# Split products of a tile pair: both wide products first, then both narrow ones

## Chip, cores and metric

One core of a Trainium2 chip runs the whole program. The metric is the device time of one execution in microseconds. Before the change the median of 3 runs is 2590.49 us (2587.98 to 2591.93).

## What is computed

A trunk of two layers over 256 positions of width 2048, in float32. Layer 0 mixes tokens with a causal Conformer convolution, layer 1 with a Mamba-2 mixer; each mixer is followed by a squared-ReLU MLP of width 8192. Cut to what matters:

```python
h = x
for i in range(2):
    sh1, sc1, g1, sh2, sc2, g2 = split(silu(c) @ w_mod[i] + b_mod[i])
    u = rmsnorm(h, norm_mix_g[i]) * (1 + sc1) + sh1
    h = h + g1 * (conformer_conv(u, ...) if i == 0 else mamba2(u, ...))
    u = rmsnorm(h, norm_mlp_g[i]) * (1 + sc2) + sh2
    r = relu(u @ mlp_w1[i])
    h = h + g2 * ((r * r) @ mlp_w2[i])
return rmsnorm(h, final_norm_g)
```

Nearly all of the work is in the large matrix products: `mlp_w1`, `mlp_w2`, the Mamba input and output projections, the Conformer's two pointwise products and `w_mod`.

## The kernel before

Activations stand transposed: channels on the 128 partitions, the T = 256 positions along the row. To keep float32 accuracy with single-pass products, a weight `w` and an activation `x` are each split into a high part (rounded to the format `F32R`) and a low part (the rest). A split activation tile holds high and low side by side, `x[:, t, :T]` and `x[:, t, T:]`, 512 columns in all. A product of a 128x128 weight tile then takes two matmuls: a wide one, high weights times both halves (512 columns), and a narrow one, low weights times the high half (256 columns), added into the right half of the same PSUM bank. The two halves of the bank are added when it is read out.

`block` computes 512 output channels from 2048 input channels. It opens 4 banks (one for each column group of 128 outputs, index `j`), and goes through 4 weight tiles of 1 MB (index `g`), each of 4 tiles of 128 input channels. `load_w` streams such a tile through SyncE's queue into one of 3 buffers `w32`. `split_w` splits it in two parts (index `i`), each of two input tiles (index `k`): ScalarE casts the high part to `wh` (line 361, 128x1024), VectorE subtracts to get `wl` (line 363). `wh` and `wl` have 3 buffers each, so ScalarE can only go on when TensorE has done with an older one. For each part and each column group TensorE then runs the products of the two input tiles, `products(...)` for `k = 0` and `k = 1`. After the second and the fourth column group `self.step()` lets waiting small jobs issue (in the Mamba layer those of the scan). After the last part `evac` reads the bank out.

With `single=True` a block writes into one half bank only: high weights times high, high weights times low, low weights times high, three matmuls of 256 columns. `block_t` (lines 430 to 432) is a third kind, with the activations as stationary operand and the weights streamed: three matmuls of 512 columns for each step. `outer` runs several blocks in step and uses `products` with `single`.

`block` without `single` runs for 13 blocks of `mlp_w1` and 3 of `mlp_w2` in layer 0, 20 blocks of the Mamba input projection (`win`), 7 of its output projection (`wout`) and 13 blocks of `mlp_w1` in layer 1: 56 blocks of 64 products.

The order on each engine is set by a scheduler of the framework: it goes by the program's order, by priorities (`high_priority`) and by when an operand should be ready, so where a weight half comes late it may run a later column group first. Only SyncE's weight stream is kept in the program's order.

Of the kernel before, what the change touches and what calls it, by code (L numbers as in the profile page):

```python
# [16 lines left out]
T = 256  # L17
# [162 lines left out]
class Trunk:  # L180
# [147 lines left out]
    def pump(self, n):  # L328
        for _ in range(n):
            if self.jobs:  # L330
                self.gemv(*self.jobs.pop(0))
        for v in self.rows_left:
            v[-1] += 1
        if self.rows_left and self.rows_left[0][-1] > WAIT:
            self.columns()
# [36 lines left out]
    def products(self, bank, w, x, k, t, cs, single, start, stop):  # L372


        def mm(out, lhsT, rhs, **kw):
            self.pe = self.nc.tensor.matmul(out, lhsT=lhsT, rhs=rhs, skip_group_check=True, **kw).ins  # L376
# [5 lines left out]
        else:  # L382
            mm(bank, wh[:, k, cs], x[:, t, :], start=start, stop=False)
            mm(bank[:, T:], wl[:, k, cs], x[:, t, :T], start=False, stop=stop)

    def block(self, src, rhs, evac, pump=None, single=False, ahead=None, after=(None, None)):


        banks = [self.bank(self.mm, "mm") for _ in range(4)]
        if single:  # L390
            banks = [v[:, :T] for v in banks]
        for g in range(4):
            w = self.load_w(src[g])
            if pump:
                with nullcontext() if g else self.tc.issue_after(self.evac):
                    self.pump(pump(g))
            with self.tc.high_priority(self.ahead if ahead is None else ahead):
                parts = self.split_w(w, (), after if g == 0 else (None, None), after[1] if g == 0 else None)
            for i, hl in enumerate(parts):
                for j in range(4):  # L400
                    cs = slice(j * P, (j + 1) * P)
                    for k in range(2):
                        t = 2 * i + k
                        self.products(banks[j], hl, rhs[g], k, t, cs, single, g == 0 and t == 0, g == 3 and t == 3)
                    if g == 3 and i == 1:
                        evac(j, [banks[j]] if single else [banks[j][:, T:], banks[j][:, :T]])
                    if j % 2:
                        self.step()
# [972 lines left out]
```

## Time and profile before

| | |
|---|---|
| runs | 2591.93, 2590.49, 2587.98 us |
| profiled execution, first to last instruction | 2591.2 us |
| TensorE matmul busy | 2540.7 us |
| TensorE weight loads busy | 2184.0 us |
| VectorE busy | 1910.9 us |
| ScalarE busy | 1311.4 us |
| GpSimd busy | 147.0 us |
| mean TensorE clock granted | 0.990 |
| moved by DMA | 664.85 MB |

The page gives no time of the profiled execution besides its span, which lies within the range of the runs. Matmuls overlap: a row of the timeline has the start and the length of a matmul, and the length reaches into the following one, so the rate of TensorE is read from the distance of starts. In the chain of work that ended last, neighbouring instructions of a line are drawn together ("x512"), and the length of such a piece is what the stretch cost. Rows called PEld are the loads of a stationary operand, which run beside the matmuls.

### The profile page before, as it was taken

How to read it: one execution, taken by the hardware profiler on the slowest of the kernel's cores; microseconds unless marked ns; L12 is line 12 of the kernel's file. 1: busy time of each engine (PE TensorE's matmuls, PEld its weight loads, DVE VectorE, ACT ScalarE, POOL GpSimd, SP SyncE). 2: the span in 40 equal slices, each digit the busy share in tenths (PEclk: the TensorE clock that was granted, in tenths of full speed). 3: DMA queues.
4: the chain of work that ended last, by engine and by line, in shares of the span. 5: the costliest groups of instructions: out<-in, count | busy, mean ns of one | idle time of the engine just before them, and what ended most of it. 6: DMA issues, size and time to landing. Idle time of an engine off the chain costs nothing.

```text
span 2591.2 us, 36890 instructions
## 1 busy us (share of the span) xinstructions
PE 2540.7 (98%) x14671; PEld 2184.0 (84%) x14671; DVE 1910.9 (74%) x2460; ACT 1311.4 (51%) x2011; POOL 147.0 (6%) x212
## 2 busy tenths in 40 slices
PE   7999999999999999999999999999999999999998
PEld 5887698988888888888888888888998888888886
DVE  6579577877878878888777777898885555565565
ACT  2067453544434434447777667744454444443443
POOL 0011000000000000000000000000001101101000
PEclk8999999999999999999999999999999999999999
DMA  9988797788888878856555455688765555555553
GB/s 404 381 322 305 266 344 300 284 326 311 313 329 316 324 287 346 320 216 221 172 194 175 167 189 194 233 310 326 294 245 192 195 181 193 194 182 194 193 184 141
DMA packets 94895, 664.85 MB, mean 257 GB/s; under 512 B 10977, under 2 KB 10977, under 8 KB 16769
## 3 DMA queue, kind: packets, MB, share of 16 engines
q1 hardware_dynamic: 89138, 643.87, 67.4%
q0 software_dynamic: 5152, 16.97, 2.4%
q8 instruction: 115, 1.88, 0.3%
q10 hardware_dynamic: 432, 1.66, 0.2%
q14 instruction: 58, 0.48, 0.0%
HBM read 657.02 MB, written 2.20 MB: 254 GB/s over the span
## 4 chain that ended last, share of the span: by engine, by line
PE 93%; DVE 3%; DMA 2%; ACT 1%; issue 1%; POOL 0%; ACTq 0%; SPq 0%; DVEq 0%
PE mm L376 58%; PE mm L430 8%; PE mm L431 8%; PE mm L432 8%; PE mm L712 7%; DMA hid<-wmT 1%; PE mm L658 1%; DVE wl L363 1%; PE ms L712 1%; DMA wm<-wmT 1%; PE ms L1293 0%; PE ms L283 0%; DMA t<-eac_d 0%; DVE hid L292 0%; ACT wh L361 0%
## 5 line engine op out<-in xcount | busy, mean ns | idle before, releaser
L376 PE MATMUL mm<-u,wh 128*128 128x512 f32 (+1 forms) x4544 | 1376.5, 365 | 4.4 <-ACT u L485 2.3
L363 DVE TENSOR_TENSOR wl<-w,wh 128x1024 fp32r<-128x1024 f32 x768 | 942.2, 1229 | 506.1 <-ACT wh L361 500.3
L361 ACT CAST wh<-w 128x1024 fp32r<-128x1024 f32 x768 | 806.1, 1050 | 975.2 <-PE mm L376 589.5
L376 PE MATMUL mm<-u,wl 128*128 128x256 f32 x3840 | 1081.0, 282 | 0.1
L376 PEld LDWEIGHTS mm<-u,wh 128*128 128x128 f32 x4544 | 812.6, 190 | 156.1 <-issue 6.6
L376 PEld LDWEIGHTS mm<-u,wl 128*128 128x128 f32 x3840 | 730.5, 190 | 5.8 <-issue 2.5
L430 PE MATMUL mm<-wh,hid 128*128 128x512 f32 x896 | 351.0, 392 | 0.0
L432 PE MATMUL mm<-wh,hid 128*128 128x512 f32 x896 | 348.9, 389 | 0.0
L431 PE MATMUL mm<-wl,hid 128*128 128x512 f32 x896 | 348.8, 389 | 0.0
L292 DVE SCALAR_TENSOR_TENSOR wm<-wm,scb 128x2048 f32<-128x2048 f32 x132 | 301.7, 2286 | 11.4 <-DMA wm<-wmT 11.2
L712 PE MATMUL mm<-u,w 128*128 128x256 f32 x864 | 191.8, 383 | 18.7 <-ACT u L586 18.7
L712 PEld LDWEIGHTS mm<-u,w 128*128 128x128 f32 x864 | 164.7, 192 | 45.1 <-ACT u L586 19.9
L430 PEld LDWEIGHTS mm<-wh,hid 128*128 128x128 f32 x896 | 168.3, 188 | 35.8 <-issue 1.0
L431 PEld LDWEIGHTS mm<-wl,hid 128*128 128x128 f32 x896 | 168.3, 188 | 35.3 <-issue 0.7
L432 PEld LDWEIGHTS mm<-wh,hid 128*128 128x128 f32 x896 | 168.3, 188 | 35.1
L376 PE MATMUL mm<-hid,wh 128*128 128x512 f32 (+1 forms) x576 | 182.3, 373 | 0.0
L376 PE MATMUL mm<-hid,wl 128*128 128x256 f32 x512 | 144.1, 281 | 0.0
L292 DVE SCALAR_TENSOR_TENSOR hid<-hid,scb 128x2048 f32<-128x2048 f32 x44 | 100.5, 2287 | 41.7 <-DMA hid<-wmT 41.5
L376 PEld LDWEIGHTS mm<-hid,wh 128*128 128x128 f32 x576 | 104.1, 189 | 20.3 <-ACT u L485 0.2
L320 POOL TENSOR_TENSOR mod<-mod,par 128x4 f32<-128x4 f32 x46 | 37.1, 806 | 1128.8 <-DVE wm L292 915.2
L605 ACT ACTIVATE taps<-u,par 128x256 f32<-128x256 f32 x224 | 93.1, 500 | 9.2 <-DVE taps L614 6.7
L376 PEld LDWEIGHTS mm<-hid,wl 128*128 128x128 f32 x512 | 97.0, 190 | 0.4 <-issue 0.2
(251 smaller groups left out, 1606.0 us busy)
## 6 DMA issues: line engine op xcount, KB each, us to landing
w<-w SPq DMA_DIRECT2D x256, 1024.0 KB, 4.9
wm<-wmT SPq DMA_DIRECT2D x139, 1024.0 KB, 7.3
w<-win SPq DMA_DIRECT2D x80, 1024.0 KB, 4.9
hid<-wmT SPq DMA_DIRECT2D x53, 1024.0 KB, 10.5
w<-pw SPq DMA_DIRECT2D x46, 1024.0 KB, 6.9
w<-wout SPq DMA_DIRECT2D x32, 1024.0 KB, 6.9
acc<-ac_d POOLq DMA_DIRECT2D x16, 512.0 KB, 8.0
xpad<-u POOLq DMA_DIRECT2D x24, 131.5 KB, 8.1
```

The source lines that it names most:

```text
L292: self.sum = nc.vector.scalar_tensor_tensor(out=w, in0=w, scalar=1.0, in1=self.scb, op0=ALU.mult, op1=ALU.mult, accum_out=m[:, i:i + 1]).ins
L320: nc.gpsimd.tensor_tensor(out=m, in0=m, in1=b, op=ALU.add)
L361: nc.scalar.copy(out=wh, in_=w[:, s, :])
L363: nc.vector.tensor_tensor(out=wl, in0=w[:, s, :], in1=wh.bitcast(F32), op=ALU.subtract)
L376: self.pe = self.nc.tensor.matmul(out, lhsT=lhsT, rhs=rhs, skip_group_check=True, **kw).ins
L430: mm(banks[q], lhsT=hi, rhs=wh[:, k, :], start=g == 0 and t == 0, stop=False)
L431: mm(banks[q], lhsT=hi, rhs=wl[:, k, :], start=False, stop=False)
L432: mm(banks[q], lhsT=lo, rhs=wh[:, k, :], start=False, stop=g == 3 and t == 3)
L605: st["tap"] = nc.scalar.activation(out=p4[:, q, :], in_=vp[:, k + q:k + q + T], func=AF.Identity, scale=self.col("w_dw", ct * TAPS + k + q ...
L658: self.pe = nc.tensor.matmul(o[32 * c:32 * c + 32, :], lhsT=w[:, k, 32 * c:32 * c + 32], rhs=r[:, c, k:k + T], start=k == 0, stop=k == 7, ...
L712: self.pe = nc.tensor.matmul(o, lhsT=w[:, t, j * P:(j + 1) * P], rhs=u[g][:, t, :], start=g == 0 and t == 0 and j < 2, stop=g == 3 and t == 3,
```

## The change

In `block`, for blocks without `single`, the four matmuls of a column group and part come in another order: the two wide ones (`k = 0` and `k = 1`), then the two narrow ones. The flags that open and close the accumulation are adapted: the first wide one of the block opens the bank, the last narrow one closes it. Blocks with `single`, `outer` and `block_t` keep their order.

```diff
+    def one_sort(self, bank, w, x, k, t, cs, lows, start, stop=False):
+
+        if lows:
+            out, lhsT, rhs = bank[:, T:], w[1][:, k, cs], x[:, t, :T]
+        else:
+            out, lhsT, rhs = bank, w[0][:, k, cs], x[:, t, :]
+        self.pe = self.nc.tensor.matmul(out, lhsT=lhsT, rhs=rhs, start=start and not lows, stop=stop and bool(lows),
+                                        skip_group_check=True).ins
+
...
-                    for k in range(2):
-                        t = 2 * i + k
-                        self.products(banks[j], hl, rhs[g], k, t, cs, single, g == 0 and t == 0, g == 3 and t == 3)
+                    if single:
+                        for k in range(2):
+                            t = 2 * i + k
+                            self.products(banks[j], hl, rhs[g], k, t, cs, single, g == 0 and t == 0, g == 3 and t == 3)
+                    else:
+                        for lows in range(2):
+                            for k in range(2):
+                                self.one_sort(banks[j], hl, rhs[g], k, 2 * i + k, cs, lows,
+                                              g == 0 and i == 0 and k == 0, g == 3 and i == 1 and k == 1)
```

On TensorE, in a `mlp_w1` block of the last MLP, before. Each row is a matmul: line, output bank, activation tile `u`, weight half `wh` or `wl`, and the shape of the output:

```order
L376 MATMUL mm_19358<-u_16268,wh_19366 128x512
L376 MATMUL mm_19358<-u_16268,wl_19367 128x256
L376 MATMUL mm_19359<-u_16268,wh_19366 128x512
L376 MATMUL mm_19359<-u_16268,wl_19367 128x256
L376 MATMUL mm_19359<-u_16268,wh_19366 128x512
L376 MATMUL mm_19359<-u_16268,wl_19367 128x256
L376 MATMUL mm_19356<-u_16466,wh_19404 128x512
L376 MATMUL mm_19356<-u_16466,wl_19405 128x256
```

The same place after the change ("x2" is two alike in a row):

```order
L392 MATMUL mm_19358<-u_16268,wh_19366 128x512 x2
L392 MATMUL mm_19358<-u_16268,wl_19367 128x256 x2
L392 MATMUL mm_19359<-u_16268,wh_19366 128x512 x2
L392 MATMUL mm_19359<-u_16268,wl_19367 128x256 x2
L392 MATMUL mm_19356<-u_16466,wh_19404 128x512 x2
L392 MATMUL mm_19356<-u_16466,wl_19405 128x256 x2
```

The second wide product of a group has moved ahead of the first narrow one; 1747 of the 1792 groups stand like this, the others are rearranged by the scheduler where a half comes late.

The scheduler also shifts work on ScalarE and VectorE. On ScalarE at the start of the Mamba layer, before; `u` is the activation tile that TensorE waits for there, `wh` a weight half of the first input blocks:

```order
L488 ACTIVATE u_9513<-nrm_9514,mod_6410 128x256
L488 ACTIVATE u_9513<-nrm_9518,mod_6410 128x256
L488 ACTIVATE u_9513<-nrm_9522,mod_6410 128x256
L488 ACTIVATE u_9513<-nrm_9526,mod_6410 128x256
L361 CAST wh_9671<-w_1451_9665 128x1024
L488 ACTIVATE u_9530<-nrm_9531,mod_6709 128x256
L488 ACTIVATE u_9530<-nrm_9535,mod_6709 128x256
L361 CAST wh_9709<-w_1456_9707 128x1024
```

The same place after:

```order
L503 ACTIVATE u_9513<-nrm_9514,mod_6410 128x256
L503 ACTIVATE u_9513<-nrm_9518,mod_6410 128x256
L361 CAST wh_9671<-w_1451_9665 128x1024
L503 ACTIVATE u_9513<-nrm_9522,mod_6410 128x256
L503 ACTIVATE u_9513<-nrm_9526,mod_6410 128x256
L503 ACTIVATE u_9530<-nrm_9531,mod_6709 128x256
L361 CAST wh_9709<-w_1456_9707 128x1024
L503 ACTIVATE u_9530<-nrm_9535,mod_6709 128x256
```

The casts go one or two activations earlier. Over the whole program ScalarE gets four more table loads, since its functions alternate a little more often.

On GpSimd, where the Mamba layer writes two small tables to memory (`ac_d`, `eac_d`) and reads the first back, before:

```order
L1204 DMA ac_d<-wm_9607 64x256
L1205 DMA eac_d<-wm_9607 64x128
L1234 DMA acc_9911<-ac_d 128x8x128
L1234 DMA acc_9912<-ac_d 128x8x128
L1234 DMA acc_10549<-ac_d 128x8x128
```

And after:

```order
L1219 DMA ac_d<-wm_9607 64x256
L1249 DMA acc_9911<-ac_d 128x8x128
L1220 DMA eac_d<-wm_9607 64x128
L1249 DMA acc_9912<-ac_d 128x8x128
L1249 DMA acc_10549<-ac_d 128x8x128
```

The write of `eac_d` has gone behind the first read of `ac_d`. SyncE's queue has the same transfers in the same order.

## Prediction

> **What bounds the kernel now.** I read the page's busy rows first, then the groups by line with shapes kept apart, then the waits of TensorE's weight loads, then the chain that ended last and the timeline inside long pieces of it.
>
> ```profile
> span 2591.2 us, 36890 instructions
> PE 2540.7 (98%) x14671; PEld 2184.0 (84%) x14671; DVE 1910.9 (74%) x2460; ACT 1311.4 (51%) x2011; POOL 147.0 (6%) x212
> L376 PE MATMUL mm<-u,wh 128*128 128x512 f32 x3136 | 1116.5, 400 | 0.4 <-ACT wh L361 0.4
> L376 PE MATMUL mm<-hid,wh 128*128 128x512 f32 x448 | 158.7, 398 | 0.0
> PEld mm L376 <- ACT u L488: 2.6, 2, 1.8
> PEld mm L376 <- ACT wh L361: 2.5, 8, 0.8
> PEld mm L376 <- DVE wl L363: 1.7, 3, 0.8
> ACT wh L361 <- PE mm L376: 589.5, 397, 4.0
> ```
>
> TensorE works through 98% of the span. Its waits on the split weights are 2.5 us (high half) and 1.7 us (low half) in all, while the engine that makes the high halves waits 589.5 us for TensorE to give buffers back. So the kernel lasts as long as TensorE's queue. The wide products of the blocks that the change touches number 3136 + 448 = 3584, each followed by a 256-column one: 3584 pairs, or 1792 groups of two pairs. What counts is the distance from the start of a pair to the start of the next, which the column of mean ns does not give (400 ns overlaps the following matmul). The chain's long pieces give it, since each is an unbroken series of L376:
>
> ```profile
> 2046.02 90.44 PE mm L376 x512
> 2401.03 90.44 PE mm L376 x512
> 1717.87 108.16 PE mm L376 x624
> 793.91 58.26 PE mm L376 x336
> 1289.60 4.24 PE mm L376 x24
> 1294.70 4.17 PE mm L376 x24
> ```
>
> The first two (start, us, matmuls) are w1 blocks of the last MLP: 90.44 / 256 pairs = 353.3 ns a pair. The third (end of the Mamba layer) is 108.16 / 312 = 346.7 ns, the fourth (first MLP) 58.26 / 168 = 346.8 ns. They are the same instructions in the same order, at two prices 6.6 ns apart, with no wait in either; I call such stretches loose (353.3) and tight (346.7). In the Mamba layer short pieces show both: 4.24 / 12 = 353 and 4.17 / 12 = 348. The timeline inside a loose and inside a tight stretch:
>
> ```profile
> 2046.20 0.40 PE L376 MATMUL mm<-u,wh 128*128 128x512 f32 x1
> 2046.43 0.28 PE L376 MATMUL mm<-u,wl 128*128 128x256 f32 x1
> 2046.55 0.40 PE L376 MATMUL mm<-u,wh 128*128 128x512 f32 x1
> 2046.79 0.28 PE L376 MATMUL mm<-u,wl 128*128 128x256 f32 x1
> 2046.91 0.40 PE L376 MATMUL mm<-u,wh 128*128 128x512 f32 x1
> ...
> 1799.86 0.39 PE L376 MATMUL mm<-u,wh 128*128 128x512 f32 x1
> 1800.09 0.28 PE L376 MATMUL mm<-u,wl 128*128 128x256 f32 x1
> 1800.21 0.39 PE L376 MATMUL mm<-u,wh 128*128 128x512 f32 x1
> ```
>
> In the loose stretch a wide product holds TensorE 230 ns one time and 240 ns the next (46.20 to 46.43, 46.55 to 46.79), a narrow one 120 ns. In the tight one it is 230 and 120 each time. Streams of one width never show the loose price:
>
> ```profile
> 2035.82 0.23 PE mm L430
> 2039.90 0.23 PE mm L430
> 1829.99 20.05 PE mm L376 x166
> 2060.21 0.28 PE L376 MATMUL mm<-u,wl 128*128 128x256 f32 x1
> 2060.21 0.19 PEld L376 LDWEIGHTS mm<-u,wh 128*128 128x128 f32 x1
> ```
>
> The first two rows are the first and last of 19 consecutive 512-column products (`block_t`, lines 430 to 432): 4.08 us over 18 steps is 226.7 ns each. The third is a block with `single`, all 256 columns wide: 20.05 / 166 = 120.8 ns. The last two show that the weights of the next product are loaded while the current one runs (both start at 2060.21), for 0.19 us; a narrow product's 0.12 us is shorter than that.
>
> **The change, part by part.** It removes nothing and adds nothing on TensorE: 3584 wide and 3584 narrow products with their weight loads. In each group it moves the second wide product ahead of the first narrow one.
>
> The step itself. Before, a group is wide, narrow, wide, narrow: 2 x 353.3 = 706.6 ns loose, 693.4 tight. After, it is wide, wide, narrow, narrow. No stretch of this order stands in the trace, so I bound it. Built from the streams of one width it is 2 x 226.7 + 2 x 120.8 = 695 ns; the tight stretch says 693.4. Nearest rows on the cheap side: coming out of a series of wide products, the first pair was quicker than any later one.
>
> ```profile
> 2045.63 0.39 PE L432 MATMUL mm<-wh,hid 128*128 128x512 f32 x1
> 2045.86 0.39 PE L376 MATMUL mm<-u,wh 128*128 128x512 f32 x1
> 2046.09 0.28 PE L376 MATMUL mm<-u,wl 128*128 128x256 f32 x1
> ```
>
> 2045.86 to 2046.20 (the next start, shown above) is 340 ns; if each group kept that once, 340 + 226.7 + 120.8 = 688 ns. Nearest rows on the dear side: one place where the scheduler happened to put two wide products, and later two narrow ones, in a row:
>
> ```profile
> 790.26 0.64 PE L376 MATMUL mm<-u,wh 128*128 128x512 f32 x2
> 790.74 0.28 PE L376 MATMUL mm<-u,wl 128*128 128x256 f32 x1
> 790.85 0.39 PE L376 MATMUL mm<-u,wh 128*128 128x512 f32 x1
> 791.08 0.40 PE L376 MATMUL mm<-u,wl 128*128 128x256 f32 x2
> 791.32 0.40 PE L376 MATMUL mm<-u,wh 128*128 128x512 f32 x1
> ```
>
> Three wide and three narrow in 1.06 us (790.26 to 791.32), 353 ns a pair: the two neighbouring wide products took 240 each, the two narrow ones 120 each. It is a single passage out of a loose stretch (and 2.6 us later the tight one of 793.91 is under way), so I take it as the dear end, not as the value. I take 693.4: half of the neighbours in the new order are of equal width, where thousands of products run without the slip, and the slip sits where a wide product follows a narrow one, which now happens once a group instead of twice.
>
> How many pairs are loose now: outside the Mamba layer's 20 input blocks (20 x 64 = 1280 pairs) there are 2304, of which the two tight rows hold 312 + 168 = 480, so 1824 loose. Of the 1280 I count half, as its short pieces show both prices; that half is an estimate. Loose 1824 + 640 = 2464, tight 1120. Gain 2464 x 6.6 ns = 16.3 us; with none of the 1280 loose 12.0, with all 20.5.
>
> The wait for the low half (`wl`). Its first reader now stands one wide product later, 0.23 us. TensorE waited for it 3 times in sum 1.7 us, so at most 3 x 0.23 = 0.7 us. Gain 0 to 0.7, I take 0.4. The second wide product needs the same `wh` as the first, so no wait is added.
>
> The buffers. `wh` gets its last reader a narrow product earlier (0.12 us), `wl` unchanged. The engine that waits for them has 589.5 us of slack; nothing, and if the cover were gone the 1.7 and 2.5 us above are what would grow.
>
> What the scheduler moved elsewhere. SyncE's queue is the same row for row, so the weight stream starts no transfer in another order. ScalarE and VectorE get the same work, some of it a few places earlier or later, and ScalarE four more table loads:
>
> ```profile
> L1244 ACT ACT_TABLE_LOAD x19 | 24.4, 1283 | 0.3
> L361 ACT CAST wh<-w 128x1024 fp32r<-128x1024 f32 x768 | 806.1, 1050 | 975.2 <-PE mm L376 589.5 <-PE mm L432 327.9 <-issue 22.2
> 1198.03 0.54 POOL L1205 DMA_DIRECT2D eac_d<-wm  x1 [1.91 <-ACT wm L1201]
> 1199.50 4.46 POOL L1234 DMA_DIRECT2D acc<-ac_d  x5 [0.93 <-DMA ac_d<-wm]
> 1230.07 1.26 POOL L1278 DMA_DIRECT2D t<-eac_d  x2 [26.12 <-ACT wh L361]
> ```
>
> Four loads of 1.28 us are 5.1 us on an engine that idles 975.2 us before its casts alone: nothing. At the start of the Mamba layer a cast of 1.05 us now goes ahead of two of the four activations that make `u`, on which TensorE waited 2.6 us in 2 waits: 0 to +2.1 us, for later casts go earlier too, 0 to -1; I take 0. On GpSimd the write of `eac_d` goes behind one read of `ac_d`: one issue of about 0.9 us (4.46 / 5) later plus the 0.93 us wait for `ac_d`, against 30 us until it is read (1230.07): nothing.
>
> Sum: -16.3 - 0.4 = -16.7 us against a span of 2591.2, that is 2574.5. The page shows no time of that execution beside its span; the span stands 0.7 us above the median of 2590.49, so about 2574 in terms of the median.
>
> **The rivals.** First, the slip is tied to each change of width, so half of it stays: 700 ns a group, 350 a pair. The loose pairs gain 3.3 (8.1 us), the tight ones lose 3.3 (3.7 us): 2586. For it: the slip follows a narrow product. Against it: the two long stretches at 346.7 with a change of width at every product.
>
> Second, the order does not matter, since the two prices belong to how a stretch starts and not to what stands in it: 2590. For it: the same instructions run at both prices. The Trainium skill (TensorE: Matmul & The Clock Gate, section "Back-to-back issue gap") gives an isolated gap of N / 2.4 + 2.5 ns, in which any order of the same four products costs the same; by it a pair would be an estimated 325 ns. The trace disagrees on the size (346.7 and 353.3) and on a single price for a width. The same page (Part 3, "What overlaps and what doesn't") lets a weight load overlap a running product only in another row group; here it overlaps with full rows, as the rows at 2060.21 show.
>
> Third, every stretch becomes loose: 353.3 for all, the tight 1120 lose 6.6 ns: +7.4 us, 2598. The passage at 790.26 speaks for it.
>
> Fourth, the other side: two narrow products in a row give the 0.19 us weight loads two short covers instead of one, the second load falls behind, and the next wide product pays a second slip of the size seen (240 against 227, 13 ns) on top of the loose group: 720 ns. Loose pairs lose 6.7 (16.5 us), tight ones 13.3 (14.9 us): 2622. It decides from the group's present mean on, (2464 x 353.3 + 1120 x 346.7) / 3584 x 2 = 702.5 ns. Against it: 166 narrow products in a row at 120.8 ns with a load each.
>
> **How the numbers follow.** Tight throughout 0.48, half 0.20, order without effect 0.10, loose throughout 0.12, a second slip 0.10. Within 0.2% (5.2 us) cannot be told from no change. Faster takes all of the first and a good third of the second with the estimate of loose pairs at its high end, 0.56; slower the last two, 0.22; the same 0.22. The likeliest case alone runs from 2570 (all Mamba pairs loose now) to 2578; the 688 ns group would give 2564 and is left out with the fourth rival, so the range is 2568 to 2598, up to the third rival.
>
> **What would show it.** Right: the pieces of 512 matmuls in the last MLP take 88.75 us instead of 90.44, and the starts inside read 227 to 230 between wide products, 120 between narrow ones. The piece of 1717.87 keeps its 346.7. Wrong: these pieces at 90.44 or above, or the 312 pairs of that piece above 108.16 us. If the pieces shrink and the time does not, the Mamba layer has lost it, and the waits on `wh`, `wl` and `u` would have grown beyond the 6.8 us they sum to.

## The result, and the profile after

The changed kernel takes 2580.67 us (median of 5 runs, 2578.43 to 2584.32), the kernel before 2590.49 (5 runs, 2587.98 to 2593.53). The ratio is 0.9961 with a 95% interval of 0.995 to 0.9971: 9.8 us less by the medians, 0.39% by the ratio. The two profiled spans differ by 9.5 us. The prediction was 2574, its range 2568 to 2598: the sign and the place were right, the gain was put at 16.7 us.

The page after, busy rows and the two groups of wide products with shapes kept apart (busy us, mean ns of one), and the waits of TensorE's weight loads (us in all, times, longest). L392 is now the line of the products whose order was changed, L376 that of the blocks with `single` and of `outer`:

```profile
span 2581.7 us, 36905 instructions
PE 2530.5 (98%) x14671; PEld 2179.4 (84%) x14671; DVE 1909.0 (74%) x2460; ACT 1316.5 (51%) x2015; POOL 147.0 (6%) x212
L392 PE MATMUL mm<-u,wh 128*128 128x512 f32 x3136 | 996.1, 399 | 0.2 <-ACT wh L361 0.2
L392 PE MATMUL mm<-hid,wh 128*128 128x512 f32 x448 | 141.6, 397 | 0.0
PEld mm L376 <- ACT u L503: 2.4, 2, 1.7
PEld mm L392 <- ACT wh L361: 1.5, 7, 0.5
PEld mm L376 <- ACT wh L361: 0.8, 1, 0.8
PEld mm L392 <- DVE wl L363: 0.2, 1, 0.2
```

TensorE still fills 98% of the span with the same 14671 products. Its busy time is 10.2 us less, though the mean of one wide product has moved by a nanosecond (400 to 399 and 398 to 397): the column of means cannot show where the time went, as the records overlap. The busy time of the groups is no help either, since two neighbours of a kind are counted once where they overlap. The waits, 6.8 us before, are 4.9; in a second execution of the changed kernel (the last experiment) the same waits sum to 6.1, so most of this moves between executions.

What shows it are the long unbroken pieces of the chain that ended last (start, us, matmuls). First those of before that the prediction did not quote, then those of after:

```profile
585.20 113.17 PE mm L376 x640
763.71 111.69 PE mm L376 x640
940.74 113.05 PE mm L376 x640
```

```profile
586.42 111.46 PE mm L392 x640
763.17 111.46 PE mm L392 x640
939.92 111.47 PE mm L392 x640
1708.85 113.56 PE mm L392 x652
2040.40 89.16 PE mm L392 x512
2216.62 89.16 PE mm L392 x512
2392.83 89.16 PE mm L392 x512
```

Divided by pairs, every one of these pieces of after gives the same: 89.16 / 256 = 111.46 / 320 = 113.56 / 326 = 348.3 ns. A group of two pairs costs 696.6 ns in all of them. Before, a pair cost 353.3 (loose) or 346.7 (tight); the piece of 763.71, 349.0 on the mean, is loose at both ends and tight between. So a loose pair gained 5.0 ns, and a tight one lost 1.6. The timeline at the entry of the last MLP, right behind `block_t`'s last product:

```profile
2040.24 0.62 PE L392 MATMUL mm<-u,wh 128*128 128x512 f32 x2
2040.69 0.40 PE L392 MATMUL mm<-u,wl 128*128 128x256 f32 x2
2040.93 0.63 PE L392 MATMUL mm<-u,wh 128*128 128x512 f32 x2
2041.40 0.39 PE L392 MATMUL mm<-u,wl 128*128 128x256 f32 x2
2041.62 0.63 PE L392 MATMUL mm<-u,wh 128*128 128x512 f32 x2
```

Two wide products take 0.45 us the first time (2040.24 to 2040.69) and 0.47 the second (2040.93 to 2041.40), two narrow ones 0.24 and 0.22. By the records' nanoseconds the groups alternate between two forms, 233, 236, 116, 112 and 233, 231, 113, 119: the wide products are slower than the 226.7 of a series of their own, the narrow ones mostly faster than 120. Read in the same way, the loose stretch of before repeats after three pairs (240 and 120, 236 and 114, 232 and 118, together 1060; the prediction took it, from a few rows, for 230 and 240 by turns with 120), and the tight one of the Mamba output after one (230 and 117).

By place, the two executions differ so (start of the same point before, then after): up to the opening block 433.88 to 435.46, +1.6, in code that the change does not touch (the granted clock was 0.89 from 305 to 320 us, against 1.00 before, and 15 x 0.11 = 1.65 us); from there to the Mamba layer -4.0 (687.19 to 683.21); the Mamba layer's input blocks -4.8 (594.94 to 590.18), where the granted clock differs too (see the Mamba input alone); its output blocks and the opening of the last MLP +1.1 (143.16 to 144.21), where before was tight; the rest -3.4 (732.03 to 728.64).

### The profile page after: what moved, and what is told of

The parts are those of the page before. It is cut to its first block, busy times and chain, and to the rows that moved or that the text cites. A ratio compares the mean times of both kernels' runs of the same rounds, so it can differ in the third digit from the quotient of the medians.

```text
span 2581.7 us, 36905 instructions
## 1 busy us (share of the span) xinstructions
PE 2530.5 (98%) x14671; PEld 2179.4 (84%) x14671; DVE 1909.0 (74%) x2460; ACT 1316.5 (51%) x2015; POOL 147.0 (6%) x212
## 4 chain that ended last, share of the span: by engine, by line
PE 93%; DVE 3%; DMA 2%; issue 1%; ACT 1%; POOL 0%; ACTq 0%; SPq 0%; DVEq 0%; POOLq 0%
PE mm L392 46%; PE mm L376 11%; PE mm L445 8%; PE mm L446 8%; PE mm L447 8%; PE mm L727 7%; DMA hid<-wmT 1%; PE mm L673 1%; DMA t<-eac_d 1%; DVE wl L363 1%; PE ms L727 1%; PE ms L283 0%; DVE a L1124 0%; PE ms L1308 0%; DVE hid L292 0%
## 5 line engine op out<-in xcount | busy, mean ns | idle before, releaser
L392 PE MATMUL mm<-u,wh 128*128 128x512 f32 x3136 | 996.1, 399 | 0.2 <-ACT wh L361 0.2
L392 PEld LDWEIGHTS mm<-u,wl 128*128 128x128 f32 x3136 | 588.1, 188 | 137.6 <-issue 0.2
L392 PE MATMUL mm<-u,wl 128*128 128x256 f32 x3136 | 617.8, 278 | 0.0
L392 PEld LDWEIGHTS mm<-u,wh 128*128 128x128 f32 x3136 | 481.2, 189 | 8.0 <-issue 4.6
L445 PE MATMUL mm<-wh,hid 128*128 128x512 f32 x896 | 350.7, 391 | 0.0
L376 PE MATMUL mm<-u,wh 128*128 128x256 f32 x1408 | 262.4, 289 | 4.2 <-ACT u L500 2.3
L376 PEld LDWEIGHTS mm<-u,wh 128*128 128x128 f32 x1408 | 224.5, 196 | 12.8 <-issue 3.4
L376 PE MATMUL mm<-u,wl 128*128 128x256 f32 x704 | 201.0, 287 | 0.0
L392 PE MATMUL mm<-hid,wh 128*128 128x512 f32 x448 | 141.6, 397 | 0.0
L376 PEld LDWEIGHTS mm<-u,wl 128*128 128x128 f32 x704 | 137.6, 196 | 1.7 <-issue 1.7
```

Source lines behind the costliest of these rows:

```text
L392: self.pe = self.nc.tensor.matmul(out, lhsT=lhsT, rhs=rhs, start=start and not lows, stop=stop and bool(lows), skip_group_check=True).ins
L445: mm(banks[q], lhsT=hi, rhs=wh[:, k, :], start=g == 0 and t == 0, stop=False)
```

## The experiments

In each, only the order of the same matmuls in `block` changes, unless said otherwise. Times stand against runs of the kernel before on the same chip: a median of 2591.28 us for the two with fewer changes of width, the one on the bank and the first on the entry; 2591.69 for the second on the entry, the two on the loads and the Mamba input alone; 2592.55 for the three sorted groups and for each part its best order; 2591.53 for the last two. H is a wide product, l a narrow one.

**Fewer changes of width.** The first theory was that each change of width costs a fixed amount. One kernel does two column groups together, HHHH then llll:

```diff
-                for j in range(4):
...
-                        for lows in range(2):
...
+                for j0 in (0, 2):
+                    for lows in range(2):
+                        for j in (j0, j0 + 1):
...
```

> Four wide products, then four narrow ones (two column groups together): half as many changes of width as in the changed kernel. Theory 'changes of width' (the extra over 346.7 ns a pair is paid where a wide product stands next to a narrow one; measured 1.6 ns a pair with one change every two products): about half the extra, 347.5 ns a pair, 88.96 us for a piece of 512 matmuls in the last MLP (89.16 in the changed kernel), and some 3 us less than the changed kernel, ratio to before about 0.995. Rival 'each order has a price of its own' (the extra is a rhythm into which an order locks, whatever the number of changes): anything from 88.75 to 90.44 us for that piece, not tied to half.

The other does a whole part, eight H then eight l:

```diff
-                for j in range(4):
...
-                        for lows in range(2):
...
+                for lows in range(2):
+                    for j in range(4):
...
```

> All eight wide products of a part first, then all eight narrow ones: a quarter of the changes of the changed kernel. Theory 'changes of width': a quarter of the extra, 347.1 ns a pair, 88.85 us a piece of 512, about 4.5 us less than the changed kernel, ratio to before about 0.9945. Rival 'each order has a price of its own': no relation to the number of changes. A second rival for the whole time: the low half is read last for longer and both halves of a part are given back at its end, so the casts start later; then the pieces shrink and the Mamba layer's waits for the split halves grow by as much.

Measured: 2588.71 us (0.9989, 0.998 to 0.9998) and 2588.16 (0.999, 0.9981 to 0.9999). A piece of the last MLP in the first kernel, then in the second, with two waits of the second:

```profile
2044.14 89.79 PE mm L392 x512
```

```profile
2042.35 89.95 PE mm L392 x512
PEld mm L392 <- DVE lo L502: 6.6, 21, 0.4
PEld mm L392 <- DVE xpad L1114: 3.3, 7, 1.8
```

The first is 350.7 ns a pair. The second reads 351.4, but it holds three ends of blocks at which two wide products take 306 and 334 ns, some 0.5 us in all; away from them eight pairs take 1841 + 953 = 2794 ns, 349.3 a pair. So with half and a quarter of the changes a pair is dearer than the 348.3 of the change itself, and of these three orders the middle one is the dearest. The theory fell. By nanoseconds, the wide products after a narrow run take 233, 236, 228, 233, 231, 227, 226, 227 in the kernel with eight: about 27 ns over eight of 226.7, spread over five products. The narrow run gives back 7 (one at 113, the rest 119 to 120). Crossing a change therefore has no fixed price; it depends on what stands around it. The second kernel also brought two kinds of wait, 9.9 us in all; that reading out four banks close together makes them is likely, and was not tested.

**The same bank.** A rival had it that the slip comes from a narrow product adding into the bank that the wide one just wrote. Two column groups are woven, so that it does so only in the first pair of a block, with H and l still alternating:

```diff
+                        if g == 0 and i == 0 and k == 0:
+                            order = [(j0, 0), (j0, 1), (j0 + 1, 0), (j0 + 1, 1)]
+                        else:
+                            order = [(j0, 0), (j0 + 1, 1), (j0 + 1, 0), (j0, 1)]
```

> Widths alternate as before, but two column groups are woven together, so that a narrow product never adds into the bank that the wide one just before it wrote: wide of group a, narrow of b, wide of b, narrow of a (only the first pair of a block keeps the plain order). Theory 'changes of width': price as before, 353.3 ns a pair, 90.4 us a piece of 512, time within 0.2% of before. Rival 'same bank' (the extra comes from adding into columns of a bank that the previous product has just written): three of four narrow products follow a wide one on another bank, so most of the extra goes, about 348 ns a pair, 89.1 us a piece, and 10 us or more less than before.

Measured: 2594.91 us (1.0009, 1.0 to 1.0018).

```profile
2045.25 90.44 PE mm L392 x512
```

This is the 90.44 of before to the last digit, though the narrow products now add into the other bank. So the bank does not make this price.

**The entry.** The prediction's second rival held that the two prices belong to how a stretch starts. The first test sorts one column group at the start of each block and alternates after that:

```diff
+                    if g == 0 and i == 0 and j == 0:
+                        order = [(0, 0), (1, 0), (0, 1), (1, 1)]
+                    else:
+                        order = [(0, 0), (0, 1), (1, 0), (1, 1)]
```

> The order of before, except that the very first column group of each block runs wide, wide, narrow, narrow. Theory 'changes of width': the rest of the block alternates and pays as before, 353.3 ns a pair, 90.4 us a piece of 512, no difference from before that can be measured (gain at most 56 groups x 10 ns = 0.6 us). Rival 'the start decides' (the same alternating order runs at 346.7 or 353.3 depending on how the stretch began; in the profile of before a stretch at 346.8 began after a passage with two wide products in a row): 88.75 us a piece, and about 16 us less than before, ratio 0.994.

Measured: 2594.99 us (1.0015, 1.0006 to 1.0024).

```profile
499.98 22.19 PE mm L392 x128
1716.31 114.49 PE mm L392 x651
2048.38 90.42 PE mm L392 x512
```

The last MLP stayed loose, so one sorted group does not do. But the block of 499.98, which follows a stream of 256-wide products, ran tight (22.19 / 64 = 346.7), and the Mamba output, tight before, ran mostly loose: it takes 0.9 us more than the changed kernel's 113.56. Prices moved though only one group in 32 had changed. So the start matters, but not in this simple way. The next kernel alternates in both MLPs, with two sorted groups at the entry of a series that follows `block_t` (none where it follows other split products, one after the opening blocks), and keeps the changed order in the Mamba layer:

```diff
+                        order = [(k, lows) for lows in range(2) for k in range(2)]
+                        if 8 * g + 4 * i + j >= sort:
+                            order = [(k, lows) for k in range(2) for lows in range(2)]
...
+                           sort=1 if not c else 2 if layer and not b else 0)
...
+                self.block(a["w2"][layer, c, b], ..., sort=2)
```

> Alternating order as before in all MLP blocks, but where a series of such blocks begins, the first column groups run wide, wide, narrow, narrow: two groups after a block_t (products all 512 wide), one group after the opening blocks (products all 256 wide). The Mamba layer's blocks keep the order of the changed kernel throughout. Theory 'entry' (the order has a repeating rhythm that the first gaps select: a group that went 233, 236, 116, 112 ns was followed by alternation at 346.7 ns, one that went 227, 227, 113, 119 by alternation at 353.3): the pieces of 512 in the last MLP take 88.8 us (89.16 in the changed kernel, 90.44 before), those of 640 in the first MLP 111.0 to 111.3, and the whole some 3 us less than the changed kernel, ratio to before 0.9945 to 0.996. Rival 'an alternating order slips sooner or later whatever its entry': pieces at 90.3 to 90.44 as before, only the Mamba layer's gain is left, ratio 0.998 to 0.9985.

Measured: 2581.17 us (0.9958, 0.9944 to 0.9971).

```profile
587.98 112.75 PE mm L392 x640
766.08 111.20 PE mm L392 x640
2040.15 88.74 PE mm L392 x512
...
2041.37 0.40 PE L392 MATMUL mm<-u,wh 128*128 128x512 f32 x1
2041.60 0.28 PE L392 MATMUL mm<-u,wl 128*128 128x256 f32 x1
2041.72 0.39 PE L392 MATMUL mm<-u,wh 128*128 128x512 f32 x1
...
612.66 0.27 PE L392 MATMUL mm<-u,wl 128*128 128x256 f32 x1
612.84 0.19 PEld L392 LDWEIGHTS mm<-u,wh 128*128 128x128 f32 x1 [0.22 <-issue]
```

Two groups in 256 pairs turn 90.44 into 88.74 (346.6 a pair, all three pieces alike): the alternation starts with steps of 232 and 118, then 231 and 112, and keeps a pair at that price for 88 us. In the first MLP the expected 111.0 to 111.3 came once of three times (the others took 112.75 and 112.17), but all three series began tight. In the first of them a weight load came late at 612.84, which held TensorE up by some 0.17 us; by the distances of starts a pair cost 346.7 ns up to there and 353.3 after it. In the other two the price went over in the same way near 862 and 988 us, where the scheduler had put wide products in a row. So in these series a price held until something broke the alternation. To see what the entry does, the same kernel with three sorted groups at that place:

```diff
-                           sort=1 if not c else 2 if layer and not b else 0)
+                           sort=1 if not c else 3 if layer and not b else 0)
```

> As e5_entry, but three instead of two groups wide, wide, narrow, narrow at the entry after a block_t in the last MLP. In the changed kernel the groups take turns between two forms after such an entry: 227, 227, 113, 119, then 233, 236, 116, 112, then 233, 231, 113, 119, and so on. Theory 'entry' (what follows depends on the form of the last group): the third group is of the form 233, 231, 113, 119, as the first was, and alternation after it is loose again, 90.4 us a piece of 512. Rival 'more groups at the entry, or any irregular start, bring the tight rhythm': 88.75 us as with two.

Measured: 2586.57 us, one run.

```profile
2039.94 90.41 PE mm L392 x512
2042.20 0.40 PE L392 MATMUL mm<-u,wh 128*128 128x512 f32 x1
2042.44 0.28 PE L392 MATMUL mm<-u,wl 128*128 128x256 f32 x1
```

Loose again, on one more sorted group. Here the second wide product of the alternation already takes 240 (2042.20 to 2042.44), where with two groups the first two took 232 and 231. Behind `block_t`, no sorted group, one (at the start of each block) and three gave loose in the last MLP; two gave tight there, and at the start of all three series of the first MLP. The four products are the same everywhere; the price goes with the form of the last sorted group: where its last narrow product took 119 ns (one group, three) the alternation ran loose, where it took 113 (two groups) tight. Why the form decides is not shown.

**The loads.** Which resource makes the rhythm? Two kernels take the order of before and, in the last MLP's w1 blocks from the second quarter on, load only 64 of the 128 stationary columns (half of the outputs is not computed there by these products): one for the narrow products, whose loads run beside a wide one, the other for the wide products, whose loads run beside a narrow one.

```diff
+        if half == lows and not start:
+            out, lhsT = out[:64], lhsT[:, :64]
...
+                           half=1 if layer and c else None)   # the other kernel: half=0
```

> Order of before. In the w1 blocks of the last MLP from its second quarter on, the narrow products load only 64 of the 128 stationary columns (half of the output channels get no low-weight product there). Theory 'short cover' (the slip comes from the load for a wide product, which has only a narrow product's 0.12 us to run beside): this load is the other one, it has a wide product's 0.23 us; the price stays 353.3 ns a pair, 90.4 us a piece of 512. Rival 'any load takes its share from the running product': half a load less, so the pair falls by 6 to 7 ns, to about 88.7 us.

> Order of before. In the w1 blocks of the last MLP from its second quarter on, the wide products load only 64 of the 128 stationary columns (half of the output channels get no high-weight product there, save the first of a block). Theory 'short cover': the load that has to run beside a narrow product is half as long, the slip goes, 346.7 ns a pair or less, 88.75 us or less a piece of 512. Rival 'any load takes its share from the running product': the same fall as with the narrow products' load halved, 6 to 7 ns a pair, to about 88.7 us; so it is the comparison of the two that tells: equal falls for the rival, a fall only here for the theory.

Measured, one run each: 2584.71 us and 2580.14. The first kernel's piece, then the second's with two of its loads:

```profile
2042.78 88.76 PE mm L394 x512
```

```profile
2042.64 87.24 PE mm L394 x512
2099.98 0.13 PEld L394 LDWEIGHTS mm<-u,wh 128*64 128x64 f32 x1
2100.09 0.19 PEld L394 LDWEIGHTS mm<-u,wl 128*128 128x128 f32 x1
```

With either load halved the slip is gone: 346.7 and 340.8 a pair against 353.3. That the first does so was not expected, since a load beside a product of 230 ns seemed to have room enough. Its 346.7 is the tight price, which alternation also reaches with whole loads, so this one run cannot tell a lighter load from another entry into the rhythm. The second price is 5.9 ns below the tight one and was seen nowhere else (its steps are 227 and 113 to 114 ns, where the tight stretch before has 230 and 117). In both kernels the product itself also uses only half of the columns, which was not tested by itself. So the loads are likely part of the rhythm, the one under the narrow product above all; it is not shown, and how a load would make a later product slip is open.

**The Mamba input alone.** The changed order only in the 20 `win` blocks, the order of before elsewhere:

```diff
+                        if 8 * g + 4 * i + j >= sort:
+                            order = [(k, lows) for k in range(2) for lows in range(2)]
...
+            self.block(a["win"][blk], ..., sort=32)
```

> The changed order only in the 20 input blocks of the Mamba layer (1280 pairs); everywhere else the order of before. It sizes the term that the prediction estimated as half of 1280. Theory 'price by pair' with half of the pairs loose before: 640 x 5.0 - 640 x 1.6 = 2.2 us, ratio 0.999; with all loose 6.4 us, ratio 0.9975. From the two profiles, the stretch from the start of the Mamba layer to its output blocks is 4.8 us shorter after the change, ratio 0.998. Rival 'the Mamba layer gains by other things than the matmuls' distance' (waits for split halves, moved jobs): the stretch shrinks by 4.8 us while the pieces of 24 and 128 matmuls in it shrink by less than half of that in sum.

Measured: 2585.49 us (0.9977, 0.9968 to 0.9986), 6.2 us less. Not all of that is the price of the new order. In the profiled executions the Mamba opening was 5.5 us shorter than before (135.25 against 140.80), and a window there shows why: length, busy us of each engine, granted clock of TensorE, share and rate of the DMA engines, before and in this kernel:

```profile
1240.00:1270.00 30.00, 27.41 (x146) 23.47 (x142) 24.73 (x41) 22.90 (x39) 1.78 (x2) 0.89 0.52 176
```

```profile
1240.00:1270.00 30.00, 29.38 (x174) 25.52 (x173) 27.93 (x48) 25.24 (x42) 0.07 (x1) 1.00 0.63 212
585.31 111.53 PE mm L392 x640
610.59 0.19 PEld L392 LDWEIGHTS mm<-u,wh 128*128 128x128 f32 x1 [0.18 <-issue]
1706.88 112.79 PE mm L392 x651
```

The granted clock was 0.89 over these 30 us before, which costs 30 x 0.11 = 3.3 us, and 1.00 in this kernel and in the changed one. Whether that belongs to the order is open: all four profiles with the order of before in these blocks (one with a sorted group at each block's start) show such a stretch in this window, 0.89 or 0.94, and none of the ten others does. The mean clock of the whole execution was 0.988 in the changed kernel's profile and 0.991 in this one's.

Another 1.6 us came in the first MLP, where nothing had changed. Its first series took 113.17 us before and 111.53 here (the second row above), in the same order: in both a weight load came late in it (at 610.49 before, at 610.59 here, the third row), and after this the series stayed loose before and ran tight here. The last row is the Mamba output, tight as before.

The steady part of the Mamba input, from 1254.75 here, is 452.13 against 454.14 before: -2.0. With the order's own 5.0 and 1.6 ns, and half of some 1056 pairs loose, 528 x 5.0 - 528 x 1.6 = 1.8 us. This fits; the share of loose pairs was not measured by itself.

**Each part its best order.** Changed order in the first MLP and the Mamba input, order of before in the Mamba output, alternation behind two sorted groups in the last MLP:

```diff
+                           sort=32 if not layer or not c else 0 if b else 2)
...
+            self.block(a["wout"][0, b], ..., sort=0)
```

> Each place gets the order that its own pieces showed cheapest: the changed order in layer 0's MLP and in the Mamba layer's input blocks, the order of before in the Mamba output blocks (112.79 us for that piece against 113.56), and in the last MLP alternation with two groups wide, wide, narrow, narrow at the entry (88.74 us a piece against 89.16). Theory 'entry': pieces 88.74 and 112.8 again, together 2.0 us less than the changed kernel, ratio to before about 0.9953. Rival 'the pieces shrink and the whole does not': ratio 0.9961 as the changed kernel.

Measured: 2582.64 us (0.9959, 0.9946 to 0.9973).

```profile
1709.81 114.95 PE mm L392 x651
2041.41 88.74 PE mm L392 x512
```

The last MLP did as expected. The Mamba output, tight in the kernel before with this very order, came out loose. The order ahead of it in the Mamba layer is not what did it: the kernel of the Mamba input alone has the same orders in the input and the output blocks, and its output ran tight (112.79). What tipped it is not shown. So the output blocks went back to the changed order, and this was timed beside the changed kernel itself:

```diff
-            self.block(a["wout"][0, b], ..., sort=0)
+            self.block(a["wout"][0, b], ...)
```

> The changed kernel, with one thing different: in the last MLP's w1 blocks from the second quarter on, a series begins with two sorted groups and alternates after that. Theory (entry decides alternation): the three pieces of 512 matmuls there read 88.74 us as in the two kernels with that entry, against 89.16 in the changed one, and nothing else moves: 3 x 0.42 = 1.3 us less, so 2579.4 against 2580.7. That is 0.05%, under what the totals can tell, so the pieces decide. Rival (what comes ahead in the Mamba layer matters too, since the kernel with this entry and 88.74 had alternation in the output blocks): pieces of 90.4, 2584.5.

> The changed kernel itself again, on the same chip as the version beside it. All theories: 2580.7 within 2, pieces of 512 matmuls at 89.16 in the last MLP and of 640 at 111.46 in the first. If the pieces differ from the first execution, the price of the sorted order depends on more than its order.

Measured: 2579.77 us (0.9954, 0.9941 to 0.9968) and 2580.91 (0.9963, 0.9951 to 0.9976). The pieces, first of the combined kernel, then of the changed one:

```profile
764.45 111.46 PE mm L392 x640
1710.44 113.56 PE mm L392 x652
2041.55 88.74 PE mm L392 x512
```

```profile
764.43 111.46 PE mm L392 x640
1709.88 113.56 PE mm L392 x652
2041.40 89.16 PE mm L392 x512
```

Every piece came as expected. In the changed kernel they repeat to 0.01 us in another execution, also where the time up to the first MLP was 1.3 us longer (587.69 against 586.42). The combined kernel is 3 x 0.42 = 1.3 us better by its pieces and 1.1 by the medians, far inside the intervals: it is the fastest measured, but only the pieces can tell.

## Why the prediction was right, and where not

- **The bound, TensorE's queue with two prices for the same pairs: right.** What the change gains steadily lies in the distances between starts; no other engine limits it, and the waits shrank by 1.9 us at most, in one execution.
- **The price of a group in the new order, taken as 693.4: wrong by 3.2 ns, and it is what mis-sized the sum.** It measured 696.6, inside the bounds of 688 and 706.6. The 695 built from streams of one width was nearer than the tight row that was chosen. The reason given, that neighbours of equal width run without a slip, failed: the wide ones take 231 to 236. That the time fell at all rests on 696.6 lying under the 702.5 of the group's mean before, which that reason did not secure; in so far the sign was luck. With the measured price the prediction's own count gives 2464 x 5.0 - 1120 x 1.6 = 10.5 us, against 9.5 between the spans and 9.8 between the medians. So the count, with half of the Mamba input loose, fits; the one term of -16.3 should have been -10.5.
- **Tight pieces keep 346.7: wrong.** The Mamba output now pays 348.3 like the other pieces, 326 x 1.6 = 0.5 us more; with the opening of the last MLP that stretch is 1.1 us longer.
- **The first rival, half of the slip kept (700 ns, 2586): as far off in its price, nearer in its time, wrong in its reason.** It missed the group by 3.4 ns, and the time by 5.3 us where 2574 missed it by 6.7. It put a fixed price on a change of width; the orders with fewer changes cost 701.5 and 698.6 a group.
- **The second rival, order without effect: wrong as a whole, but half of it was the core.** Alternation has no price of its own: its entry, and what breaks it on the way, decide. The sorted order has one (348.3 in all seven pieces above). The formula for an isolated gap in the Trainium skill (TensorE: Matmul & The Clock Gate, section "Back-to-back issue gap") depends on the number of columns alone, so by it every order of the same products would cost the same. The traces disagree: 346.7, 348.3, 349.3, 350.7 and 353.3 a pair.
- **The two rivals on the dear side: neither came.** None of the sorted order's long pieces cost 353.3 a pair or more.
- **The small terms: right in the main.** The wait on `wl` went from 1.7 to 0.2 us, 1.5 less where at most 0.7 was allowed; in the second execution of the changed kernel it was 1.0, so this is the size of what moves between executions. The wait on `u` went from 2.6 to 2.4, so the cast ahead of it cost nothing. ScalarE has 4 instructions more, as counted, and is not waited for longer.
- **What the prediction did not have:** stretches at a reduced clock, 3.3 us in the Mamba opening before and 1.6 us ahead of the opening block after, and a price of alternation that can go over in the middle of a series. They are the size of the spread between runs and cancel only in part, so the agreement of 10.5 with 9.5 should not be read to the microsecond.

## What to carry to other kernels

Where a queue is full, price a product by the distance between starts over a long unbroken piece, not by its recorded duration, and look whether the same instructions have two prices in the same trace: then the order, or what precedes it, is worth trying. Prefer an order whose price does not depend on its entry to one that is slightly cheaper when it starts well. When the price of a new order is not in the trace, a mean of the streams it is built from can be a better guess than the best stretch of another order; here it was 695 against 693.4, and 696.6 was measured.

## What the hardware showed that was not expected

- A rhythm can lock, and one late load can change it. An alternation of 512- and 256-column products with a weight load for each ran 256 pairs at 346.7 or at 353.3 ns, without a wait in either, as two or three sorted groups stood ahead of it. In the first MLP a load that was late by 0.2 us turned a tight series loose (at 612.84) and in another kernel a loose one tight (at 610.59).
- What an order costs over long runs of one width (226.7 for a wide product, 120 for a narrow one) comes in steps of about 6.6 ns for a repeat: two groups of the sorted order 1393.1 against 1386.7, one step; three loose pairs 1060 against 1040, three; sixteen products in fours 2805.9 against 2773.3, five; sixteen in eights 2794, three. Why is open.
- With 64 stationary columns instead of 128 for the narrow products a pair ran at 346.7 instead of 353.3, with 64 for the wide ones at 340.8. The recorded times of the loads (0.13 and 0.19 us in the second kernel) do not say why.
